# Two transformer blocks on one core: TensorE's instructions of the expert stage issued in the order of the code

## The chip, the cores and the metric

The kernel runs on one core of one Trainium2 chip. A core has five engines, each with an instruction queue that it works through in order: PE (TensorE: matrix products; its weight loads are shown as PEld), DVE (VectorE), ACT (ScalarE), POOL (GpSimd) and SP (SyncE, which here issues all loads from memory). They wait for each other through semaphores. The metric is the device time of one execution in microseconds (us), as the median of several runs.

## The reference, cut to what matters

Two blocks work on 256 tokens of 1024 features: first a block of two mixers followed by a mixture of 32 experts, then two attention layers with feed-forward parts. The change lies in the experts, where each token goes to 2 of 32:

```python
    expert = g_idx * EXPERTS_PER_GROUP + e_idx
    ...
    xb = x_pad[tok_buf].reshape(n_blocks, MOE_BLOCK, D)

    def expert_block(args):
        xbk, e = args
        return (jax.nn.silu(xbk @ w_gate[e]) * (xbk @ w_up[e])) @ w_down[e]

    yb = lax.map(expert_block, (xb, block_e)).reshape(P, D)
    y = jnp.zeros((N + 1, D), yb.dtype).at[tok_buf].add(yb * w_buf[:, None].astype(yb.dtype))
```

`w_gate` and `w_up` of one expert are 1024 x 512, `w_down` is 512 x 1024, all in 32-bit floats: 6 MiB for each expert, 192 MiB for all of them, and every expert is computed.

## The kernel before, in words

**Work of the expert stage.** Experts are taken in 16 pairs `j`; each expert has 64 token slots, so that a pair fills 128 rows. Expert `a` of a pair (0 or 1) takes columns 64a to 64a+63 of the array, and the two can run side by side. The parts are:

- `gather(quad)`, once for two pairs (four experts): picks the tokens by products with one-hot matrices `D4` (made by DVE, L1190): 32 matmuls of L1198 into eight PSUM tiles, which ACT (L1202) and DVE (L1204) scale into `xg`.
- `widen(j)`, twice for a pair (gate, then up): 16 matmuls of L1216, of which each takes 64 columns; it uses four weight tiles of 1 MiB, two for each half of the sum.
- `gated(j)`: ACT's silu of the gate product (L1222); the product with the up half is DVE's L1307.
- `turned(j)`: four transposes (L1230) of the hidden values, copied by ACT.
- `places(j)`: two transposes (L1240) and two small products (L1245) for the way back.
- `narrow(j)`: 16 matmuls of L1261 with the `down` weights (four tiles of 1 MiB), and behind them the drains: DVE scales (L1269), ACT rounds (L1270), DVE makes the rest (L1271). The results are `oh` and `ol`.
- `scatter(j)`: eight matmuls (L1280 with `oh`, L1282 with `ol`) that add a pair's result to four PSUM tiles `yp`.

Each of these 32-bit matmuls of L1216 and L1261 is two records in the trace.

**Order.** The code is a software pipeline over `j`: in the step of pair `j` it writes `gather` (for even `j`), gate half of `j`, `turned(j-1)`, `scatter(j-2)`, `places(j-1)`, up half of `j`, `narrow(j-1)`. But the code's order isn't the order on the engine: a scheduler at build time takes instructions by priority as it thinks that they come ready, and so sets the order in each queue anew. A block under `tc.manual_schedule(engines=...)` keeps the written order on the engines named.

**Groups.** Pairs 0 to 9 and 10 to 15 are two groups. Between them stands `crowded()`, a conditional block for an expert with more than 64 tokens: each engine reads a number and branches, and no instruction is moved across it. The block isn't entered with these inputs.

**Weights.** All loads are 1 MiB, issued by SP in the order of use that the code states: gate(j), up(j), down(j-1), four tiles each. 18 tiles are issued ahead of the stage; 14 of their places are then used in turn, and a further load waits for the matmuls that last read the place it is to fill, and for the load eight before it. Four of the 18 (`EARLY`) lie in buffers that the stage itself uses later; using them up starts no further load. 192 tiles are loaded in all. After them SP issues loads for the next block.

Of the kernel before, what the change touches and what calls it, by code (L numbers as in the profile page):

```python
# [16 lines left out]
OP = mybir.AluOpType  # L17
# [9 lines left out]
MORE = 2  # L27
GROUPS = (range(0, 10), range(10, 16))

EARLY = {4: "em", 3: "ay", 11: "oo", 17: "xg"}  # L30
ORDER = (0, 1, 2, 5, 6, 7, 8, 9, 10, 3, 4, 11, 12, 13, 14, 15, 16, 17)

FILL_A = (0, 0, 2, 8, 0, 2)
# [12 lines left out]
_E = mybir.EngineType  # L46
# [13 lines left out]
def block(ctx, tc, A, out, dbg=None):  # L60
    nc = tc.nc
    PE, ACT, DVE, POOL, SP = nc.tensor, nc.scalar, nc.vector, nc.gpsimd, nc.sync
# [111 lines left out]
    modc = const.tile([128, 18, 8], F32, name="modc")  # L174
# [255 lines left out]
    def bcast_cols(dst, c):  # L430

        for n in range(2):
            p = pmm()
            for a in range(4):
                PE.matmul(p[:, 128 * a:128 * a + 128], c[:, 4 * n + a:4 * n + a + 1].to_broadcast([128, 128]), ident,  # L435
                          start=a == 0, stop=a == 3, skip_group_check=True)
            ACT.activation(dst[:, 512 * n:512 * n + 512], p, AF.Copy)


    with ExitStack() as c1:  # L440
# [401 lines left out]
        op = []  # L842
# [103 lines left out]
    with ExitStack() as c2:  # L946
# [3 lines left out]
        big = lambda n: pool.tile([128, D], F32, name=n, tag="big", bufs=1)  # L950
# [144 lines left out]
        for j in ORDER:  # L1095
            rings[:] = [partial(pool.tile, tag=EARLY[j], bufs=1 + (EARLY[j] == "xg")) if j in EARLY else next(rest)]
            ahead[j] = first[j]()
# [79 lines left out]
        em = pool.tile([128, 4, 512], F32, name="em")  # L1177
        ay = pool.tile([128, 4, 512], F32, name="ay")
# [6 lines left out]
        fp = lambda t: t.rearrange("s (p f) -> s f p", f=4)  # L1185

        def gather(quad):
            D4 = pool.tile([128, 2, 4, 64], F32R, name="D4", bufs=2)
            for i in range(2):
                DVE.tensor_tensor(D4[:, i], pos[:, i, 4 * quad:4 * quad + 4, None].to_broadcast([128, 4, 64]),  # L1190
                                  slot[:, None, :].to_broadcast([128, 4, 64]), op=OP.is_equal)
            xg = pool.tile([128, KT, 256], F32, name="xg", bufs=2)
            for kt in range(KT):
                p = pmm()
                n = 0
                for i in range(2):
                    for hx in (xh, xl):
                        PE.matmul(p[:, 0:256], hx[:, i, 128 * kt:128 * kt + 128],  # L1198
                                  D4[:, i].rearrange("p e s -> p (e s)"), start=n == 0, stop=n == 3)
                        n += 1  # L1200
                if kt % 2:
                    ACT.activation(xg[:, kt, :], p[:, 0:256], AF.Identity, scale=G2r[:, kt:kt + 1], bias=S2r[:, kt:kt + 1])  # L1202
                else:
                    DVE.tensor_scalar(xg[:, kt, :], p[:, 0:256], G2r[:, kt:kt + 1], S2r[:, kt:kt + 1], op0=OP.mult, op1=OP.add)  # L1204
            S_["quad", quad] = D4, xg

        def widen(j):

            xg = S_["quad", j // 2][1]
            p = pmm()  # L1210
            for n in range(2):
                wt = [staged_moe() for a in range(2)]
                for k in range(4):
                    kt = 4 * n + k
                    for a in range(2):
                        PE.matmul(p[64 * a:64 * a + 64, :], xg[:, kt, lc(2 * j + a)], wt[a][:, k, :], start=kt == 0,  # L1216
                                  stop=kt == KT - 1, skip_group_check=True)
            return p

        def gated(j, p):  # L1220
            a4 = ac2[j % 2].rearrange("s (f p) -> s f p", f=4)
            ACT.activation(a4, fp(p), AF.Silu)  # L1222
            if j == 15:
                act_set(LNEXP)
            return a4

        def turned(j):
            p = pmm()
            for f in range(4):
                PE.transpose(p[:, 128 * f:128 * f + 128], ac2[j % 2][:, 128 * f:128 * f + 128], ident)  # L1230
            hT = hT2[j % 2].rearrange("p (f s) -> p f s", f=4)
            ACT.activation(hT, p.rearrange("p (f s) -> p f s", f=4), AF.Copy)

        def places(j):
            D4 = S_["quad", j // 2][0]
            pr_ = j % 2
            Dp = [D4[:, i, 2 * pr_:2 * pr_ + 2, :].rearrange("p e s -> p (e s)").bitcast(F32) for i in range(2)]
            p = pmm()
            for i in range(2):
                PE.transpose(p[:, 128 * i:128 * i + 128], Dp[i], ident)  # L1240
            DT = pool.tile([128, S], F32R, name="DT", bufs=2)
            ACT.activation(DT, p[:, 0:S], AF.Copy)
            p = pmm()
            for i in range(2):
                PE.matmul(p[:, 0:2], Dp[i], Wt[:, i, 2 * j:2 * j + 2], start=i == 0, stop=i == 1)  # L1245
            wsl = pool.tile([128, 1], F32, name="wsl", bufs=2)
            for a in range(2):
                DVE.tensor_copy(wsl[64 * a:64 * a + 64], p[64 * a:64 * a + 64, a:a + 1])
            S_["pair", j] = DT, wsl

        def narrow(j):
            wsl = S_["pair", j][1]
            hT = hT2[j % 2].rearrange("p (f s) -> p f s", f=4)
            pd = [pmm(), pmm()]
            for f2 in range(2):
                wt = [staged_moe() for a in range(2)]
                for b in range(2):
                    f = 2 * f2 + b
                    for n in range(2):
                        for a in range(2):  # L1260
                            PE.matmul(pd[n][64 * a:64 * a + 64, :], hT[:, f, 64 * a:64 * a + 64],  # L1261
                                      wt[a][:, b, 512 * n:512 * n + 512], start=f == 0, stop=f == 3,
                                      skip_group_check=True)
            o = pool.tile([128, 2, D], F32R, name="o", tag="oo")
            oh, ol = o[:, 0, :], o[:, 1, :]
            for n in range(2):
                ns = slice(512 * n, 512 * n + 512)
                yf = yf2[n]
                DVE.scalar_tensor_tensor(yf, pd[n], wsl, ga2[:, ns], op0=OP.mult, op1=OP.mult)  # L1269
                ACT.activation(oh[:, ns], yf, AF.Copy)  # L1270
                DVE.tensor_tensor(ol[:, ns], yf, oh[:, ns].bitcast(F32), op=OP.subtract)  # L1271
            S_["out", j] = oh, ol

        def scatter(j):
            DT = S_["pair", j][0]
            oh, ol = S_["out", j]
            for n in range(2):
                ns = slice(512 * n, 512 * n + 512)
                for i in range(2):
                    PE.matmul(yp[i][n], DT[:, 128 * i:128 * i + 128], oh[:, ns], start=j == 0, stop=False,  # L1280
                              skip_group_check=True)
                    PE.matmul(yp[i][n], DT[:, 128 * i:128 * i + 128], ol[:, ns], start=False, stop=j == 15,  # L1282
                              skip_group_check=True)
            if j == 12:

                for i in range(2):
                    for n in range(2):
                        PE.matmul(yp[i][n], ident, x_sb[:, i, 512 * n:512 * n + 512], start=False, stop=False,
                                  skip_group_check=True)
                bcast_cols(fnb, colr("fng", 8))  # L1290

        for g in GROUPS:

            before, done2 = None, None
            for j in [*g, None]:
                if j is not None:
                    if j % 2 == 0:
                        gather(j // 2)
                    a4 = gated(j, widen(j))
                if before is not None:  # L1300
                    turned(before)
                if done2 is not None:
                    scatter(done2)
                if before is not None:
                    places(before)
                if j is not None:
                    DVE.tensor_tensor(a4, a4, fp(widen(j)), op=OP.mult)  # L1307
                if j == 0:
                    ga2 = big("ga2")
                    bcast_cols(ga2, modc[:, 5, :])  # L1310
                if before is not None:
                    narrow(before)
                done2, before = before, j
            scatter(g[-1])
            if g[0] == 0:
                crowded()
        rings[:] = [slots(ring)]
# [33 lines left out]
    with ExitStack() as c3:  # L1351
# [88 lines left out]
        for ly in range(2):  # L1440
# [208 lines left out]
            for f2 in range(11):  # L1649
# [3 lines left out]
                for b in range(2):  # L1653
# [9 lines left out]
                    g, u = pgu  # L1663
# [86 lines left out]
```

## Time and profile before

| | |
|---|---|
| three runs, median | 1465.2 us (1461.68 to 1467.49) |
| the profiled execution, its own time | 1462.69 us |
| its span, first to last instruction | 1460.9 us |
| mean granted clock of TensorE | 0.981 |
| PE busy | 1376.7 us (94%) |
| DVE, ACT, POOL busy | 765.2 us, 575.1 us, 77.1 us |
| moved by the loads | 400.42 MB |
| L1216 (gate and up) | 1024 records, from 275.8 us to 725.1 us |
| L1261 (down) | 512 records, from 306.4 us to 746.0 us |

A busy PE need not be at its peak: records overlap, and a stretch counts as busy also where only one of the two column halves works. The expert stage reaches from about 270 us to about 750 us, a third of the span.

### The profile page before, as it was taken

How to read it: one execution, taken by the hardware profiler on the slowest of the kernel's cores; microseconds unless marked ns; L12 is line 12 of the kernel's file. 1: busy time of each engine (PE TensorE's matmuls, PEld its weight loads, DVE VectorE, ACT ScalarE, POOL GpSimd, SP SyncE). 2: the span in 40 equal slices, each digit the busy share in tenths (PEclk: the TensorE clock that was granted, in tenths of full speed). 3: DMA queues.
4: the chain of work that ended last, by engine and by line, in shares of the span. 5: the costliest groups of instructions: out<-in, count | busy, mean ns of one | idle time of the engine just before them, and what ended most of it. 6: DMA issues, size and time to landing. Idle time of an engine off the chain costs nothing.

```text
span 1460.9 us, 22923 instructions
## 1 busy us (share of the span) xinstructions
PE 1376.7 (94%) x9330; PEld 994.1 (68%) x9330; DVE 765.2 (52%) x1507; ACT 575.1 (39%) x1020; POOL 77.1 (5%) x79
## 2 busy tenths in 40 slices
PE   6989999799999998999979989999998999999997
PEld 5878877443443433434338867899997897799997
DVE  5648758311211111111155985888876575766665
ACT  3543014310110111101146764555556586645444
POOL 1003000100000000000010230000020001100000
PEclk9999999799999999999999999999999999999999
DMA  9926589599999999999936573878775533555540
GB/s 357 300 76 231 178 298 421 200 402 415 427 428 426 426 384 416 427 426 395 402 119 231 202 258 131 294 274 308 291 247 189 176 129 137 194 190 196 181 155 30
DMA packets 138687, 400.42 MB, mean 274 GB/s; under 512 B 6561, under 2 KB 84657, under 8 KB 114002
## 3 DMA queue, kind: packets, MB, share of 16 engines
q1 hardware_dynamic: 138578, 398.91, 71.1%
q8 instruction: 75, 1.23, 0.3%
q14 instruction: 34, 0.28, 0.1%
HBM read 397.82 MB, written 1.05 MB: 273 GB/s over the span
## 4 chain that ended last, share of the span: by engine, by line
PE 53%; DVE 3%; ACT 3%; issue 2%; POOL 0%; POOLq 0%; DVEq 0%; ACTq 0%
PE pmm L416 8%; PE pmm L417 8%; PE pmm L418 8%; PE pmm L1216 6%; PE pacc L416 5%; PE pacc L417 5%; PE pacc L418 5%; PE pmm L1261 2%; PE pmm L190 1%; PE pmm L1198 1%; PE pmm L435 1%; PE pmm L366 1%; DVE x_sb L1408 1%; PE pmm L1618 1%; PE pacc L1531 1%
## 5 line engine op out<-in xcount | busy, mean ns | idle before, releaser
L416 PE MATMUL pmm<-hh,whi 128*128 128x256 f32 (+1 forms) x1040 | 295.4, 284 | 2.0 <-ACT whi L167 2.0
L418 PE MATMUL pmm<-hh,wlo 128*128 128x256 f32 (+1 forms) x1040 | 296.2, 285 | 0.2 <-DVE wlo L168 0.2
L417 PE MATMUL pmm<-hl,whi 128*128 128x256 f32 (+1 forms) x1040 | 294.6, 283 | 0.0
L1216 PE MATMUL pmm<-wruns,xg 128*64 128x512 f32 x1024 | 237.1, 595 | 0.0
L168 DVE TENSOR_TENSOR wlo<-wcols,whi 128x1024 fp32r<-128x1024 f32 (+1 forms) x130 | 168.3, 1299 | 97.5 <-ACT whi L167 97.1
L416 PEld LDWEIGHTS pmm<-hh,whi 128*128 128x128 f32 (+1 forms) x1040 | 196.9, 189 | 8.5 <-issue 3.6
L417 PEld LDWEIGHTS pmm<-hl,whi 128*128 128x128 f32 (+1 forms) x1040 | 196.1, 189 | 1.4
L418 PEld LDWEIGHTS pmm<-hh,wlo 128*128 128x128 f32 (+1 forms) x1040 | 196.4, 189 | 0.6 <-DVE wlo L168 0.4
L167 ACT ACTIVATE whi<-wcols 128x1024 fp32r<-128x1024 f32 (+1 forms) x130 | 136.0, 1052 | 116.3 <-PE pmm L417 89.1
L1216 PEld LDWEIGHTS pmm<-wruns,xg 128*64 128x64 f32 x1024 | 73.9, 137 | 141.3 <-issue 139.2
L1261 PE MATMUL pmm<-wruns,em 128*64 128x512 f32 x512 | 138.4, 596 | 0.0
L168 DVE TENSOR_TENSOR wlo<-wrows,whi 128x1024 fp32r<-128x1024 f32 x87 | 108.1, 1249 | 56.6 <-ACT whi L167 56.2
L167 ACT ACTIVATE whi<-wrows 128x1024 fp32r<-128x1024 f32 x87 | 91.6, 1061 | 92.3 <-PE pmm L417 46.7
L1307 DVE TENSOR_TENSOR ay<-ay,pmm 128x512 f32<-128x512 f32 x16 | 11.0, 688 | 184.6 <-PE pmm L1216 184.6
L1261 PEld LDWEIGHTS pmm<-wruns,em 128*64 128x64 f32 x512 | 44.0, 137 | 73.5 <-issue 71.0
L1270 ACT ACTIVATE o<-ay 128x512 fp32r<-128x512 f32 x32 | 20.1, 629 | 160.1 <-DVE ay L1269 160.1
L417 PE MATMUL pacc<-wlo,ah 128*128 128x512 f32 x176 | 69.2, 393 | 0.0
L416 PE MATMUL pacc<-whi,ah 128*128 128x512 f32 x176 | 68.9, 391 | 0.0
L418 PE MATMUL pacc<-whi,al 128*128 128x512 f32 x176 | 68.6, 393 | 0.0
L1269 DVE SCALAR_TENSOR_TENSOR ay<-pmm,wsl,ga 128x512 f32<-128x512 f32 x32 | 24.0, 751 | 82.9 <-PE pmm L1261 81.2
L1202 ACT ACTIVATE xg<-pmm,GS 128x256 f32<-128x256 f32 x32 | 18.0, 562 | 88.0 <-PE pmm L1198 78.2
L1222 ACT ACTIVATE ay<-pmm 128x512 f32<-128x512 f32 x16 | 9.6, 598 | 108.9 <-PE pmm L1216 108.9
(533 smaller groups left out, 2198.8 us busy)
## 6 DMA issues: line engine op xcount, KB each, us to landing
wruns<-in_moe_w_gate_dram SPq DMA_DIRECT2D x64, 1024.0 KB, 11.7
wruns<-in_moe_w_up_dram SPq DMA_DIRECT2D x64, 1024.0 KB, 13.5
wruns<-in_moe_w_down_dram SPq DMA_DIRECT2D x64, 1024.0 KB, 13.6
wrows<-in_w_mod_dram SPq DMA_DIRECT2D x48, 1024.0 KB, 7.2
wcols<-in_w_ffn_gate_dram SPq DMA_DIRECT2D x22, 1024.0 KB, 5.1
wcols<-in_w_ffn_up_dram SPq DMA_DIRECT2D x22, 1024.0 KB, 7.4
wrows<-in_w_ffn_down_dram SPq DMA_DIRECT2D x22, 1024.0 KB, 5.2
wrows<-in_ada_w_dram SPq DMA_DIRECT2D x16, 1024.0 KB, 7.4
```

Of the source, the lines that this page charges most:

```text
L167: ACT.activation(hi, src, AF.Copy)
L168: (POOL if ahead else DVE).tensor_tensor(lo, src, hi.bitcast(F32), op=OP.subtract)
L190: PE.matmul(p[32 * g:32 * g + 32, 0:n].rearrange("p (a j) -> p a j", j=32), lhsT, groups(rhs)[:, g], start=first, stop=last, skip_group_ch ...
L366: PE.matmul(p, src[:, i, 128 * kt:128 * kt + 128], dg[i], start=True, stop=True)
L416: PE.matmul(p, a[0], b[0], start=first, stop=False, skip_group_check=True)
L417: PE.matmul(p, a[0], b[1], start=False, stop=False, skip_group_check=True)
L418: PE.matmul(p, a[1], b[0], start=False, stop=last, skip_group_check=True)
L1202: ACT.activation(xg[:, kt, :], p[:, 0:256], AF.Identity, scale=G2r[:, kt:kt + 1], bias=S2r[:, kt:kt + 1])
L1216: PE.matmul(p[64 * a:64 * a + 64, :], xg[:, kt, lc(2 * j + a)], wt[a][:, k, :], start=kt == 0, stop=kt == KT - 1, skip_group_check=True)
L1261: PE.matmul(pd[n][64 * a:64 * a + 64, :], hT[:, f, 64 * a:64 * a + 64], wt[a][:, b, 512 * n:512 * n + 512], start=f == 0, stop=f == 3, ski ...
L1269: DVE.scalar_tensor_tensor(yf, pd[n], wsl, ga2[:, ns], op0=OP.mult, op1=OP.mult)
L1270: ACT.activation(oh[:, ns], yf, AF.Copy)
```

## The change

All of TensorE's instructions of the two group loops stand under `manual_schedule`, so they are issued as written. The code is written in another order, too: the `gather` of the next two pairs stands between the up half of an odd pair and the `narrow` ahead of it (before, ahead of the gate half of an even pair); in a group's last step `turned` comes behind `scatter` and `places`. Of the loads issued ahead, tile 12 instead of tile 17 lies in the second `xg` buffer, since that buffer is now filled before tile 17 is used.

```diff
-EARLY = {4: "em", 3: "ay", 11: "oo", 17: "xg"}
+EARLY = {4: "em", 3: "ay", 11: "oo", 12: "xg"}
...
         for g in GROUPS:
 
-            before, done2 = None, None
-            for j in [*g, None]:
-                if j is not None:
-                    if j % 2 == 0:
-                        gather(j // 2)
-                    a4 = gated(j, widen(j))
-                if before is not None:
-                    turned(before)
-                if done2 is not None:
-                    scatter(done2)
-                if before is not None:
-                    places(before)
-                if j is not None:
-                    DVE.tensor_tensor(a4, a4, fp(widen(j)), op=OP.mult)
-                if j == 0:
-                    ga2 = big("ga2")
-                    bcast_cols(ga2, modc[:, 5, :])
-                if before is not None:
-                    narrow(before)
-                done2, before = before, j
-            scatter(g[-1])
+            with tc.manual_schedule(engines={_E.PE}):
+                before, done2 = None, None
+                gather(g[0] // 2)
+                for j in [*g, None]:
+                    if j is not None:
+                        a4 = gated(j, widen(j))
+                        if before is not None:
+                            turned(before)
+                    if done2 is not None:
+                        scatter(done2)
+                    if before is not None:
+                        places(before)
+                    if j is not None:
+                        DVE.tensor_tensor(a4, a4, fp(widen(j)), op=OP.mult)
+                    else:
+                        turned(before)
+                    if j == 0:
+                        ga2 = big("ga2")
+                        bcast_cols(ga2, modc[:, 5, :])
+                    if before is not None:
+                        if j is not None and j % 2 and j + 1 in g:
+                            gather((j + 1) // 2)
+                        narrow(before)
+                    done2, before = before, j
+                scatter(g[-1])
             if g[0] == 0:
                 crowded()
```

What stands in PE's queue in the middle of the first group, before the change, where the next quad is gathered (`D` is the one-hot matrix, `em` the transposed hidden values, `ay` the hidden values; each "..." is 8 to 10 more rows of L1198 of the same kind):

```order
L1216 MATMUL pmm<-wruns,xg 64x512 x31
L1261 MATMUL pmm<-wruns,em 64x512 x2
L1198 MATMUL pmm<-D_3885,xh 128x256
...
L1261 MATMUL pmm<-wruns,em 64x512 x6
...
L1261 MATMUL pmm<-wruns,em 64x512 x2
...
L1261 MATMUL pmm<-wruns,em 64x512 x6
...
L1280 MATMUL pacc<-o,DT 128x512 x2
L1216 MATMUL pmm<-wruns,xg 64x512
L1230 MATMUL pmm<-ident,ay 128x128 x4
L1282 MATMUL pacc<-o,DT 128x512 x2
```

The gate half of the next pair stands with the up half of this one (31 of 32 together, one behind the drains), and `narrow` is cut into four pieces with `gather` between them. The same engine at the same place in the program, with the change ("..." is the rest of the 32 rows of L1198):

```order
L1216 MATMUL pmm<-wruns,xg 64x512 x16
L1198 MATMUL pmm<-D_3854,xh 128x256
...
L1261 MATMUL pmm<-wruns,em 64x512 x16
L1216 MATMUL pmm<-wruns,xg 64x512 x16
L1230 MATMUL pmm<-ident,ay 128x128 x4
L1280 MATMUL pacc<-o,DT 128x512
L1282 MATMUL pacc<-o,DT 128x512
```

Up half, gather, `narrow` and the next gate half now stand each in one piece, and in the order in which their weights are loaded. Within each piece the two column halves alternate from matmul to matmul, as the code writes them; before, the scheduler had put two matmuls of the same half one behind the other in most of `narrow`.

The second place is ACT's queue at the end of the stage, where the last pair's results are rounded (L1270) and the first weights of the next block are split (L167). Before:

```order
L1242 ACTIVATE DT<-pmm 128x256
L1270 ACTIVATE o<-ay 128x512 x4
L167 ACTIVATE hilo<-wrows 128x1024 x2
L294 ACTIVATE sqj,ssx_5374<-pacc 128x512
L294 ACTIVATE sqj,sst_5376<-tf 128x512
```

And with the change:

```order
L1232 ACTIVATE em<-pmm 128x512
L1270 ACTIVATE o<-ay 128x512
L167 ACTIVATE hilo<-wrows 128x1024
L1270 ACTIVATE o<-ay 128x512
L167 ACTIVATE hilo<-wrows 128x1024
L294 ACTIVATE sqj,ssx_5380<-pacc 128x512
```

One split of the next block's weights now stands between the two last roundings.

## Rows read from the trace of the kernel before

**Rows 1.** The page, 40 equal slices of the span: GB/s moved by the loads.

```profile
GB/s 357 300 76 231 178 298 421 200 402 415 427 428 426 426 384 416 427 426 395 402 119 231 202 258 131 294 274 308 291 247 189 176 129 137 194 190 196 181 155 30
```

**Rows 2.** Stretches: length, busy PE, PEld, DVE, ACT, POOL (instructions); clock, DMA share, GB/s.

```profile
280.00:300.00 20.00, 20.00 (x106) 8.36 (x104) 0.72 (x2) 2.93 (x6) 0.00 (x0) 1.00 0.93 347
300.00:320.00 20.00, 20.00 (x107) 9.24 (x107) 5.57 (x11) 3.69 (x8) 0.00 (x0) 1.00 1.01 420
320.00:340.00 20.00, 20.00 (x99) 8.05 (x97) 1.76 (x5) 1.53 (x3) 0.00 (x0) 1.00 0.99 397
433.73:493.63 59.90, 58.39 (x261) 23.81 (x260) 10.52 (x20) 7.72 (x15) 0.00 (x0) 1.00 1.01 426
540.00:560.00 20.00, 15.90 (x60) 5.96 (x56) 6.35 (x10) 2.52 (x4) 0.00 (x0) 1.00 0.82 334
...
680.00:700.00 20.00, 20.00 (x90) 7.93 (x87) 0.31 (x2) 2.07 (x4) 0.00 (x0) 1.00 0.85 327
716.00:736.00 20.00, 19.47 (x88) 7.06 (x84) 1.75 (x4) 2.75 (x4) 0.00 (x0) 1.00 0.87 363
```

**Rows 3.** Timeline of PE, start and duration, first pairs, whose pieces stand whole.

```profile
275.83 13.95 PE L1216 MATMUL pmm<-wruns,xg 128*64 128x512 f32 x64
...
341.55 7.04 PE L1216 MATMUL pmm<-wruns,xg 128*64 128x512 f32 x32
...
358.45 7.09 PE L1261 MATMUL pmm<-wruns,em 128*64 128x512 f32 x32
365.47 0.39 PE L1198 MATMUL pmm<-D,xh 128*128 128x256 f32 x1
...
369.72 3.65 PE L1216 MATMUL pmm<-wruns,xg 128*64 128x512 f32 x16
```

**Rows 4.** Timeline of PE in the middle of the first group (brackets: idle before, releaser).

```profile
433.73 13.52 PE L1216 MATMUL pmm<-wruns,xg 128*64 128x512 f32 x61
...
455.25 0.73 PE L1280 MATMUL pacc<-o,DT 128*128 128x512 f32 x2 [0.71 <-ACT o L1270]
...
476.12 3.65 PE L1261 MATMUL pmm<-wruns,em 128*64 128x512 f32 x12
...
493.63 13.52 PE L1216 MATMUL pmm<-wruns,xg 128*64 128x512 f32 x61
```

**Rows 5.** Timeline of PE's weight loads in the same quad.

```profile
462.08 0.14 PEld L1216 LDWEIGHTS pmm<-wruns,xg 128*64 128x64 f32 x2 [0.29 <-issue]
...
478.31 0.14 PEld L1261 LDWEIGHTS pmm<-wruns,em 128*64 128x64 f32 x1 [0.29 <-issue]
...
483.24 0.19 PEld L1198 LDWEIGHTS pmm<-D,xh 128*128 128x128 f32 x1 [0.81 <-issue]
```

**Rows 6.** Timeline of SP, the issue of loads at the end of the stage.

```profile
718.47 0.39 SPq L143 DMA_DIRECT2D wrows<-in_w_qkv_dram  x1
719.31 3.80 SPq L143 DMA_DIRECT2D wrows<-in_w_mod_dram  x3
```

**Rows 7.** Timeline of PE and ACT between the groups and at the end.

```profile
556.68 0.63 PE L1282 MATMUL pacc<-o,DT 128*128 128x512 f32 x2
...
563.38 0.55 PE L1198 MATMUL pmm<-D,xh 128*128 128x256 f32 x1 [6.06 <-PEq L1120]
...
569.27 14.81 PE L1216 MATMUL pmm<-wruns,xg 128*64 128x512 f32 x66
...
739.98 7.09 PE L1261 MATMUL pmm<-wruns,em 128*64 128x512 f32 x30
...
748.43 1.99 ACT L167 ACTIVATE hilo<-wrows 128x1024 fp32r<-128x1024 f32 x2
```

**Rows 8.** A stretch between the groups (columns as in rows 2).

```profile
562.00:564.00 2.00, 0.62 (x3) 0.65 (x4) 0.76 (x2) 0.00 (x0) 0.00 (x0) 0.50 1.00 422
```

**Rows 9.** Single instruction lines: the identity products of the second group, L1288 and L435.

```profile
L1288 PE MATMUL pacc<-x_sb,ident x8: 592/592/697, 678.7 to 686.6; 128*128 128x512 f32 x8
L435 PE MATMUL pmm<-ident,par x16: 275/275/376, 690.7 to 692.5; 128*128 128x128 f32 x16
```

## The prediction

> **What bounds the kernel now.** First the slices of the page [rows 1]: in the expert stage (from the ninth slice to the twentieth) the loads run at 384 to 428 GB/s, nowhere else for so long; the dips among these are what to look at. The stretches [rows 2] then show both sides at once: in one quad (two pairs) from 433.73 to 493.63 us PE is busy for 58.39 of 59.90 us, while the loads move 426 GB/s at a share of 1.01. So neither waits visibly for the other, and the question is which of them is only filled up.
>
> The timeline of PE answers it. Early in the stage, where each part stands whole, a pair takes 23.92 us (341.55 to 365.47), and a gather up to 4.25 us (365.47 to 369.72, with one scatter product in it) [rows 3]. Two pairs and a gather would be 52.1 us. In the middle of the group the same work takes 59.90 us [rows 4]: 7.8 us more. The loads of 24 tiles (24 x 1.0486 MB = 25.17 MB) at 426 GB/s take 59.1 us. PE is thus 0.8 us slower than the loads in a quad, with 7.8 us that aren't work. Where they go is read from the weight loads [rows 5]: in L1216 two go in each 0.43 us, one for each column half; in the cut `narrow` of L1261 most come singly at the same step, so one half of the array stands idle, and at each change between 64 and 128 columns 0.81 us pass. That is why twelve shown records of L1261 take 3.65 us [rows 4], where 32 take 7.09 [rows 3]. In each pair PE also waits 0.71 us for ACT's L1270, the first drain of `narrow`, since scatter comes right behind it [rows 4].
>
> At the end the slower one shows: from 716 to 736 us the loads move 363 x 20 = 7.26 MB [rows 2], 6.9 tiles, of which the last four are the next block's [rows 6]. So 2.9 tiles of the experts are left at 716, and the last lands at about 716 + 2.9 x 2.46 = 723 us. PE ends its last `narrow` at 739.98 + 7.09 = 747.07 us [rows 7], 24 us later. Loads also fell short twice because the places weren't freed: 334 GB/s in 540 to 560 and 327 in 680 to 700, which is 4.3 and 4.7 us of loads at 426 [rows 2].
>
> **The change, part by part.**
>
> *PE's work.* Nothing is added or removed: the same matmuls in another order. The clean pair of [rows 3] is the new order, piece by piece, with no wait in it, so I take 23.92 us for a pair; in the new place the gather's results have the whole `narrow` (7.0 us) to reach `xg`, and ACT and DVE are mostly idle there (10.52 and 7.72 us busy of 59.90 [rows 2]). A gather of 4.2 us is the upper value, 3.9 without the scatter product. Waits that the trace doesn't show in this order: at least 0 (the clean pair), at most the 0.71 us of [rows 4] in each pair, 11 us in all. I take 0, since scatter now stands a whole gate half (7.0 us) behind the drain that it waited for.
>
> PE alone would then run: from 275.83 us [rows 3], ten pairs 239.2, four gathers 16.8, the broadcast beside pair 0 about 2 and the last drain 3: group one ends at 537. Group two is six pairs (143.5), two gathers (8.4) and the identity products, eight records at 0.43 us and sixteen in 1.8 (together 5.6) [rows 9]: 157.5 us.
>
> *The loads.* All 192 tiles must still come, and they can't come faster than at about 426 GB/s: 2.46 us each. By 340 us the loads have moved (347 + 420 + 397) x 20 = 23.28 MB, 22.2 tiles [rows 2], which with the 18 issued ahead leaves 151.8. At 2.46 us they take 373.6 us: 713.6 us, if they never stop. One new stop I count: the first gather of the loop (4.2 us) now stands ahead of the first `narrow`, so the places of tiles 16 and 17 come free 4.2 us later. It costs 0 if enough loads are queued to cover it, and 4.2 if none are; no row shows the queue there, so I take the middle, 2.1. That gives 715.7.
>
> Is PE ahead of this? Tile 119, the last of group one, is the 79.8th of these and lands at 340 + 2.1 + 79.8 x 2.46 = 538.4 us; PE alone would be done by then. From there: a landing delay of 1 us (I bound it by 0 and 2), half a `narrow` (3.5), the drains (about 3), then 11.96 us from the last scatter through the branch to the first L1216 (557.31 to 569.27 [rows 7]): 557.9. With 157.5 us of work PE would end at 715.4, while the loads need half a `narrow` behind the last tile: 715.7 + 1 + 3.5 = 720.2 us. The loads decide, by some 5 us, and PE's waits below 0.8 us a pair in group two cost nothing. The pause at the branch is covered: 14 places are 34 us of loads.
>
> *The end.* ACT's L167 now stands between the last two L1270: 1.0 us [rows 7], of which nothing hides most, because the last scatter waits for the second. I take 1.0 (bounds 0 and 1.0; if its load is late, 2.5 more). What follows, the next block, starts when `narrow` and its drains are done, and moves as a whole.
>
> *Two edits at nothing.* `turned` behind `scatter` in a group's last step: the same five short matmul groups, covered by the wait for tiles there. The buffer of tile 12 instead of 17: one place fewer, none more.
>
> **Sum.** 747.07 - 720.2 - 1.0 = 25.9 us. The profiled execution's own 1462.69 us becomes 1436.8; it lies 2.5 us under the median of the runs, so for the median 1439.3, say **1439 us**. The stop (0 to 4.2), the landing (0 to 2), the last L167 (0 to 3.5) and a GB/s or two move this by 4 us down and 6 up: 1435 to 1445.
>
> The Trainium skill, in DMA: Bandwidth & Descriptors (Where 436 GB/s comes from), puts the ceiling of the loads at 435 GB/s, and says that for loads from memory about 358 bind. By 435 the 151.8 tiles would take an estimated 366 us and the end would come 7.7 us earlier; by 358 they would take 445 us. The trace disagrees with 358 (426 over a whole quad) and reaches 428 in a slice at most [rows 1].
>
> **The rivals.**
>
> *PE still waits in its new order.* The scheduler had moved the gate half ahead for a reason, perhaps for drains. If each pair has 1.5 us of waits (twice the 0.71 of [rows 4]), group one ends at 537 + 15 = 552, 6 us after what the loads allow (538.4 + 7.5), and group two is 9 us longer: 715.4 + 15 = 730.4 instead of 720.2: 1449 us. Against it: the clean pair shows none. Chance 0.15.
>
> *The loads were the limit all along.* For it: 426 GB/s for whole quads. Then only the two dips go, 9.0 us: 1456 us. Against it: PE ends 24 us behind the last tile. Chance 0.08.
>
> *The wait for tiles slows PE's clock (slower than before).* PE will now wait for tiles, by (59.1 - 52.1) / 12 = 0.6 us for each half of a part. After 6.06 us without work [rows 7] the granted clock stood at 0.50, 1.2 GHz instead of 2.4 [rows 8]. If that came with the short waits, the three 7 us parts of a pair would take 14 each: 21 us more for each pair so slowed. Two such pairs cost 42 us, and the result is 1439 + 42 = 1481 us; from (25.9 + 7.3) / 21 = 1.6 pairs on it is more than 0.5% slower. Against it: with waits of 0.71 us in each pair the clock stayed at 1.00 [rows 2]. Chance 0.03. The Trainium skill, in TensorE: Matmul & The Clock Gate (HAM oscillation — how this bites in real kernels), tells of a kernel whose waits for each weight slice brought the slow clock back every time; here the waits are shorter than any that the trace shows at 0.50.
>
> *The loads run faster than 426 once PE never holds them.* With 434 GB/s 151.8 tiles take 366.8 us, 6.8 less: 1432 us, with PE 2 us behind them. Chance 0.06.
>
> **How the numbers follow.** My forecast has 0.68. Range: 1431 takes in the faster loads and the lower bounds, 1453 the new waits; left out are the dips alone (0.08), the slow clock (0.03) and some tails: about 0.17. The likeliest case's own range is the 1435 to 1445 above. About 0.5%, 7.3 us, is what a measurement of this kernel tells from no change: under 1457.9 lie the forecast, the waits, the faster loads and most of the 0.08: 0.94 faster, 0.03 the same, 0.03 slower.
>
> **What would show it.** In the changed kernel's trace: weight loads of L1261 in twos at 0.43 us; pairs of about 24 us up to roughly 460 us and then quads at 59 us, PE waiting on loads of `wruns` rather than on L1270; no dip in the loads from 345 us to the end of the stage; PE's last `narrow` ending 3 to 5 us behind the last tile, near 720 us. Wrong would be: a quad above 60 us, loads below 420 GB/s in the middle, waits of PE on ACT or DVE of more than 0.8 us a pair, or a clock below 1.00 inside a group.

## The result

1442.44 us, median of four runs (1441.75 to 1445.49), against 1465.4 us before (1461.68 to 1467.49, four runs): a ratio of 0.985, with a 95% interval of 0.9826 to 0.9875, some 23 us gained. The prediction of 1439 us, with its range of 1431 to 1453, was right. The traced execution is the slowest of the four (1445.49 us, its span 1443.7), and reaches the experts 3 us later than that of before: the first L1216 starts at 278.81 us, not 275.83. So positions are compared from the first L1216 on, and I call "the stage" the time from there to the first L366 of the next block: 481.9 us before (757.71 - 275.83), 462.1 after (740.91 - 278.81), a gain of 19.8 us. The rest of the two spans differs by 2.6 us the other way, in work that the change doesn't touch.

### The profile page after: what moved, and what is told of

It reads as the page before. It is cut to its first block, busy times and chain, and to the rows that moved or that the text cites. A ratio compares the mean times of both kernels' runs of the same rounds, so it can differ in the third digit from the quotient of the medians.

```text
span 1443.7 us, 22926 instructions
## 1 busy us (share of the span) xinstructions
PE 1356.1 (94%) x9330; PEld 1002.3 (69%) x9330; DVE 763.9 (53%) x1507; ACT 576.5 (40%) x1020; POOL 77.9 (5%) x79
## 4 chain that ended last, share of the span: by engine, by line
PE 44%; DMA 9%; DVE 3%; ACT 3%; issue 1%; POOL 0%; POOLq 0%; DVEq 0%; SPq 0%; ACTq 0%
PE pmm L416 8%; PE pmm L417 8%; PE pmm L418 8%; PE pacc L416 5%; PE pacc L417 5%; PE pacc L418 5%; DMA wruns<-in_moe_w_gate_dram 4%; DMA wruns<-in_moe_w_down_dram 3%; DMA wruns<-in_moe_w_up_dram 2%; PE pmm L190 1%; PE pmm L1261 1%; ACT sqj L294 1%; PE pmm L366 1%; PE pmm L1622 1%; PE pmm L435 1%
## 5 line engine op out<-in xcount | busy, mean ns | idle before, releaser
L1216 PE MATMUL pmm<-wruns,xg 128*64 128x512 f32 x1024 | 233.1, 595 | 7.1 <-DMA wruns<-in_moe_w_gate_dram 7.1
L168 DVE TENSOR_TENSOR wlo<-wcols,whi 128x1024 fp32r<-128x1024 f32 (+1 forms) x130 | 168.4, 1300 | 99.3 <-ACT whi L167 98.8
L167 ACT ACTIVATE whi<-wcols 128x1024 fp32r<-128x1024 f32 (+1 forms) x130 | 136.1, 1053 | 119.0 <-PE pmm L417 91.7
L1216 PEld LDWEIGHTS pmm<-wruns,xg 128*64 128x64 f32 x1024 | 81.8, 137 | 141.1 <-issue 115.8
L168 DVE TENSOR_TENSOR wlo<-wrows,whi 128x1024 fp32r<-128x1024 f32 x87 | 108.1, 1248 | 56.3 <-ACT whi L167 55.9
L167 ACT ACTIVATE whi<-wrows 128x1024 fp32r<-128x1024 f32 x87 | 91.7, 1061 | 90.5 <-PE pmm L417 45.5
L1261 PE MATMUL pmm<-wruns,em 128*64 128x512 f32 x512 | 118.4, 595 | 7.2 <-DMA wruns<-in_moe_w_down_dram 5.7
L1261 PEld LDWEIGHTS pmm<-wruns,em 128*64 128x64 f32 x512 | 38.5, 137 | 79.3 <-issue 62.4
L1270 ACT ACTIVATE o<-ay 128x512 fp32r<-128x512 f32 x32 | 20.2, 631 | 177.5 <-DVE ay L1269 177.5
L1248 DVE COPY wsl<-pmm 64x1 f32<-64x1 f32 x32 | 5.0, 156 | 130.7 <-PE pmm L1245 130.4
```

The lines of the kernel that those rows point to most:

```text
L167: ACT.activation(hi, src, AF.Copy)
L168: (POOL if ahead else DVE).tensor_tensor(lo, src, hi.bitcast(F32), op=OP.subtract)
```

## The profile after

The slices of the page, GB/s moved by the loads, to be held against [rows 1]:

```profile
GB/s 361 295 69 251 164 274 380 226 365 426 426 427 426 427 427 402 391 426 427 427 246 252 196 228 146 336 276 311 286 248 181 172 117 149 184 196 196 178 150 30
```

From the tenth slice to the twentieth one dip is left, 402 and 391. Before there were two, 384 and 395.

PE's timeline early in the stage (start, duration), which answers to [rows 3]:

```profile
320.79 7.04 PE L1216 MATMUL pmm<-wruns,xg 128*64 128x512 f32 x32
327.76 0.66 PE L1230 MATMUL pmm<-ident,ay 128*128 128x128 f32 x4
...
330.76 7.09 PE L1216 MATMUL pmm<-wruns,xg 128*64 128x512 f32 x32
337.68 7.04 PE L1261 MATMUL pmm<-wruns,em 128*64 128x512 f32 x32
344.54 7.04 PE L1216 MATMUL pmm<-wruns,xg 128*64 128x512 f32 x32
...
365.55 7.09 PE L1261 MATMUL pmm<-wruns,em 128*64 128x512 f32 x32
372.47 4.03 PE L1216 MATMUL pmm<-wruns,xg 128*64 128x512 f32 x18
```

All pieces stand whole (the x18 of the last row is only where this view ends). A pair takes 23.75 us (320.79 to 344.54), one with a gather 27.93, a quad 51.68. Further on PE waits for loads, first at 453 us:

```profile
447.90 4.62 PE L1216 MATMUL pmm<-wruns,xg 128*64 128x512 f32 x18
453.74 3.65 PE L1216 MATMUL pmm<-wruns,xg 128*64 128x512 f32 x14 [1.21 <-DMA wruns<-in_moe_w_gate_dram]
```

The stretches of the core (columns as in [rows 2]): two with waits for loads, the stop between the groups, and the end.

```profile
500.00:520.00 20.00, 16.41 (x77) 6.82 (x74) 3.10 (x6) 2.83 (x5) 0.00 (x0) 1.00 1.01 426
...
560.00:580.00 20.00, 20.00 (x103) 13.71 (x103) 2.32 (x4) 2.60 (x5) 0.00 (x0) 0.99 0.82 335
680.00:700.00 20.00, 20.00 (x93) 7.59 (x89) 3.48 (x5) 2.10 (x4) 0.00 (x0) 1.00 1.01 427
```

In 500 to 520 PE is busy for 16.41 us only, at clock 1.00. The dip at 680 to 700 (327 before) is gone; the one between the groups, 334 before, is still there with 335. Its cause is in SP's queue. These are the instructions of the branch line L1120 (count, duration in ns, first and last start), before:

```profile
L1120 SPq EVENT_SEMAPHORE  x8: 17/17/17, 531.7 to 546.5; - x8
L1120 SPq COMPARE_BRANCH  x1: 50/50/50, 529.4 to 529.4; - x1
```

and after:

```profile
L1120 SPq EVENT_SEMAPHORE  x8: 17/17/17, 575.5 to 578.3; - x8
...
L1120 PEldq COMPARE_BRANCH  x1: 6126/6126/6126, 551.2 to 551.2; - x1
L1120 PEldq EVENT_SEMAPHORE  x1: 51/51/51, 557.3 to 557.3; - x1
L1120 SPq COMPARE_BRANCH  x1: 50/50/50, 559.3 to 559.3; - x1
```

SP compares at 559.3 and gets past the eight semaphores at 578.3. They are those of its eight outstanding loads: as the program is written, SP leaves the conditional block only when every load that it has issued has landed. The landing times in the trace agree: before, the loads issued from 523.03 to 529.06 us land at 539.18, 541.61, 544.03 and 546.45, and a wait of SP ends within 0.02 us of each. The queue of loads runs dry and starts anew. Before, this lasted from 529.4 to 546.5. The prediction had taken that dip for places that weren't free. (PE passes a branch of its own here, which takes 6.1 us, and 6.0 before.)

The end of the stage on PE (answers to [rows 7]):

```profile
715.16 3.65 PE L1261 MATMUL pmm<-wruns,em 128*64 128x512 f32 x14 [1.14 <-DMA wruns<-in_moe_w_down_dram]
719.51 0.49 PE L1280 MATMUL pacc<-o,DT 128*128 128x512 f32 x1 [0.71 <-ACT o L1270]
720.25 0.50 PE L1282 MATMUL pacc<-o,DT 128*128 128x512 f32 x1 [0.24 <-DVE o L1271]
...
722.57 0.64 PE L1230 MATMUL pmm<-ident,ay 128*128 128x128 f32 x4
723.89 7.09 PE L1261 MATMUL pmm<-wruns,em 128*64 128x512 f32 x32 [0.69 <-ACT em L1232]
731.70 0.51 PE L1280 MATMUL pacc<-o,DT 128*128 128x512 f32 x1 [0.72 <-ACT o L1270]
...
735.65 0.80 PE L1282 MATMUL pacc<-o,DT 128*128 128x512 f32 x1 [1.98 <-DVE o L1271]
```

The last wait for a load ends at 715.16. Behind it come half a `narrow`, `scatter`, `places`, `turned` and a whole `narrow`, with three waits for drains (0.71, 0.24, 0.69). The last `narrow` ends at 730.98. DVE's last L1271 comes late:

```profile
731.73 0.68 DVE L1271 TENSOR_TENSOR o<-ay,o 128x512 fp32r<-128x512 f32 x1
732.99 0.69 DVE L1333 TENSOR_TENSOR tf<-pacc,em 128x512 f32<-128x512 f32 x1 [0.59 <-PE pacc L1282]
733.60 1.99 DVE L1271 TENSOR_TENSOR o<-ay,o 128x512 fp32r<-128x512 f32 x1
```

It takes 1.99 us in place of 0.68, beside POOL's split of the next block's weights (L168, 732.67 to 737.82).

## The experiments

**How they are read.** The theory: PE's new order frees it, and from then on the loads bound the stage; what is left to gain are stops of the loads and the chain at the end. Repeated runs of one kernel lie up to 6.5 us apart (the kernel before: 1459.53 to 1466.03), and chips differ a little, so that medians tell some 3 us from nothing; smaller steps are read from the stage of the traced execution, one for each kernel.

| kernel | median, us | ratio to before, 95% | stage, us |
|---|---|---|---|
| before | 1465.4 | | 481.9 |
| after | 1442.4 | 0.9826 to 0.9875 | 462.1 |
| e1_fixed_old | 1439.6 | 0.9817 to 0.9870 | 459.1 |
| e2_order_only | 1453.0 | 0.9902 to 0.9955 | 471.1 |
| e3_fewer_loads | 1418.3 | 0.9671 to 0.9723 | 436.5 |
| e4_halves_apart | 1449.1 | 0.9876 to 0.9929 | 469.0 |
| e5_no_branch | 1440.8 | 0.9822 to 0.9848 | 457.4 |
| e6_pool_loads | 1440.1 | 0.9816 to 0.9843 | 457.9 |
| e7_tail | 1445.9 | 0.9860 to 0.9890 | 462.1 |
| e8_gather1 | 1441.6 | 0.9826 to 0.9854 | 461.4 |
| e9_old_pool | 1440.3 | 0.9817 to 0.9843 | 458.9 |
| e10_old_pool_split | 1442.4 | 0.9830 to 0.9862 | 459.7 |
| e11_turned_first | 1444.6 | 0.9849 to 0.9881 | 461.8 |
| e12_old_pool_at | 1438.3 | 0.9815 to 0.9844 | 458.7 |

**One part alone: the fixed order (e1_fixed_old).** The loop of before, put under `manual_schedule`:

```diff
+            with tc.manual_schedule(engines={_E.PE}):
                 before, done2 = None, None
                 for j in [*g, None]:
```

> TensorE's instructions of the expert stage in the order written, but the code in its old order: each gather ahead of the gate half of an even pair, `turned` ahead of `scatter` in a group's last step, tile 17 in the early buffer. Theory (the gain is the whole pieces of `narrow` and the alternating column halves, and from the middle on the loads bound the stage, so that where the gather stands is covered): 1442 us, 1440 to 1446. Rival (the gather between the pair's two halves is what gains): 1450 to 1465.

1439.6 us. The fixed order alone gives the whole gain. The other edits gain nothing on top of it: the stage is even 3.0 us shorter than after's. Part of that is early: over the first 60 us of the stage the loads average 359 GB/s, 349 in after (from 20 to 40 us 408 for 358), which is 1.4 us of loads. Where the rest comes from stays open.

**The other part alone (e2_order_only).** The code of after without the `with`.

> The code in its new order, but the scheduler still free to set TensorE's queue. It cuts `narrow` again: 48 places where two matmuls of the same column half follow each other (52 in the kernel before, none after). Theory: 1455 to 1466, most of the gain gone. Rival (the new place of the gather gains): 1440 to 1450.

1453.0 us, better than expected: half the gain. The scheduler still cuts pieces and hoists part of the gate half, but now the gather cuts `widen` into three pieces and leaves `narrow` whole: a pair with its gather takes 31.42 us (462.79 to 494.21) against 34.18 before (459.45 to 493.63) and 27.93 after; one without takes the same 25.7 us as before. PE never waits for loads here. So PE bounds this kernel, and the new code order is worth about 12 us while the scheduler is free, and nothing once the order is fixed.

**Is it the loads? (e3_fewer_loads).** The second half of `narrow` uses the tiles of the first:

```diff
-        dn_runs = lambda j: [... for f2 in range(2) for a in range(2)]
+        dn_runs = lambda j: [... for f2 in range(1) for a in range(2)]
...
-                wt = [staged_moe() for a in range(2)]
+                wt = wt if f2 else [staged_moe() for a in range(2)]
```

> The kernel after, with a sixth of the experts' loads left out: the second half of each `narrow` computes with the tiles of its first half again, so the result is another one. TensorE's instructions are the same. Theory (the loads at 426 GB/s bound the second half of the stage, TensorE alone would be some 13 us faster: 7.1 us of waits for loads at L1216 and 5.7 at L1261 in the profile after): 1429 us, 1425 to 1433. Rival (TensorE waits for something that goes with the places or the branch, not with the bytes): 1438 to 1444.

1418.3 us: 24 us less with the same instructions on PE, so the loads do bound the kernel after, and by twice what was expected. The groups of lines show why, after first, then this kernel (busy us, mean ns of one | idle before):

```profile
L1216 PE MATMUL pmm<-wruns,xg 128*64 128x512 f32 x1024 | 233.1, 595 | 7.1 <-DMA wruns<-in_moe_w_gate_dram 7.1
L1261 PE MATMUL pmm<-wruns,em 128*64 128x512 f32 x512 | 118.4, 595 | 7.2 <-DMA wruns<-in_moe_w_down_dram 5.7 <-ACT em L1232 1.4
```

```profile
L1216 PE MATMUL pmm<-wruns,xg 128*64 128x512 f32 x1024 | 225.5, 594 | 0.0
L1261 PE MATMUL pmm<-wruns,em 128*64 128x512 f32 x512 | 113.0, 594 | 1.4 <-ACT em L1232 1.4
```

Beside the 12.8 us of idle time before records, 13.0 us of "busy" are gone (233.1 + 118.4 - 225.5 - 113.0). A wait for a tile within a piece is partly shown as busy PE: at 453.74 us PE shows 1.21 us of idle time, its weight load 2.09. In the stage of after the weight loads show 28.2 us of idle time ended by loads, in 19 gaps that otherwise take 0.29 us each. The two parts on PE are 25.8 us together; the stage got 25.6 shorter.

**The column halves (e4_halves_apart).**

```diff
-                for b in range(2):
-                    f = 2 * f2 + b
-                    for n in range(2):
-                        for a in range(2):
+                for a in range(2):
+                    for b in range(2):
+                        f = 2 * f2 + b
+                        for n in range(2):
```

> The kernel after, with only the loops within `narrow` exchanged: four matmuls of one column half, then four of the other, instead of alternating. Same matmuls, whole pieces, no cut. Theory (two neighbours on different halves run side by side, two on the same half do not): 13 steps of 0.87 us in place of 8, so a `narrow` takes 11.3 us in place of 7.1; 16 x 4.3 = 69 us more, less the 13 us that TensorE now waits for loads: 1498 us, 1480 to 1510. Rival (the cutting and the changes between 64 and 128 columns cost the time, not the halves): 1441 to 1446.

1449.1 us, 7 more and not 56: the theory of this experiment fell, and so did its rival. PE's timeline where `narrow` meets the next gate half:

```profile
338.34 7.63 PE L1261 MATMUL pmm<-wruns,em 128*64 128x512 f32 x29
345.39 0.64 PE L1216 MATMUL pmm<-wruns,xg 128*64 128x512 f32 x1
345.81 0.59 PE L1261 MATMUL pmm<-wruns,em 128*64 128x512 f32 x1
...
346.73 7.40 PE L1216 MATMUL pmm<-wruns,xg 128*64 128x512 f32 x29
354.06 0.66 PE L1230 MATMUL pmm<-ident,ay 128*128 128x128 f32 x4
```

One half is ahead by a few records and goes on into the gate half, while the other finishes `narrow`. The two run side by side all the same. The lag is paid once, where work of 128 columns follows, as the weight loads show:

```profile
463.13 0.14 PEld L1216 LDWEIGHTS pmm<-wruns,xg 128*64 128x64 f32 x1 [0.29 <-issue]
463.56 0.14 PEld L1216 LDWEIGHTS pmm<-wruns,xg 128*64 128x64 f32 x1 [0.29 <-issue]
463.99 0.14 PEld L1216 LDWEIGHTS pmm<-wruns,xg 128*64 128x64 f32 x1 [0.29 <-issue]
464.94 0.14 PEld L1230 LDWEIGHTS pmm<-ident,ay 128*128 128x128 f32 x1 [0.81 <-issue]
```

A pair (from L1230 to L1230) takes 25.63 us (328.43 to 354.06) for 23.75 in after (327.76 to 351.51): 1.9 us, not 4.3. Sixteen times 1.88 us on the stage of e3_fewer_loads, where PE doesn't wait for loads, is 436.5 + 30.1 = 466.6 us; measured 469.0. So same-half neighbours need not cost anything by themselves: they leave one half behind, and PE pays for that where the piece ends. That each cut in the kernel before is paid in this way is concluded, not measured: no run cuts the pieces and keeps the halves alternating.

**The branch (e5_no_branch, e6_pool_loads).** In the first the call of `crowded()` is left out; in the second

```diff
-                ahead.append(t())
+                ahead.append(t(q=POOL) if 120 <= k < 132 else t())
```

> The kernel after without the conditional block `crowded()` between the groups (it isn't entered with these inputs). Theory (SP's branch waits for the landing of all its outstanding loads, so the queue of loads runs empty and starts anew, some 4.5 us of loads, and the stage is bound by loads): 4.5 us less than the kernel after, 3 to 7, no dip in the loads near 580 us. Rival (the dip comes from places that are not free; the branch itself is covered): 0 to 1 us less, the dip stays.

> The kernel after, with the twelve loads that follow SP's branch issued by POOL, which has passed its own branch before the stage begins. Theory (loads can go on while SP waits at the branch for its own to land): the dip near 580 us goes, 3 to 5 us less than the kernel after. Rival (the queue empties all the same since both queues share the engines and end together, or POOL's issue is slower): 0, or up to 5 us more.

The stage is 4.7 and 4.2 us shorter than after's, as expected for the stop. The medians are only 1.6 and 2.4 less, short of the expected 3 to 7 and 3 to 5; they point the same way, but can't tell it from nothing. From 280 to 300 us into the stage the loads of after move 356 GB/s; here are the same 20 us without the branch, then with POOL's loads:

```profile
558.35:578.35 20.00, 20.00 (x98) 8.00 (x96) 1.00 (x3) 2.06 (x4) 0.00 (x0) 1.00 1.01 428
```

```profile
554.99:574.99 20.00, 20.00 (x104) 9.59 (x105) 2.87 (x5) 2.86 (x5) 4.43 (x8) 0.95 1.01 424
```

SP still sat at its branch in the second (555.6 to 581.5), and the loads didn't stop. So the stop is SP's branch, which waits for the landing of its own loads. e5_no_branch also takes away PE's own 6.1 us at the branch; e6_pool_loads keeps them (5.9 us) and gains nearly as much, so it isn't they that count.

**The tail (e7_tail, e11_turned_first).** In e7 the last step of a group is `turned`, `places`, `narrow` and then both scatters; in e11 only `turned` moves back ahead of `scatter` and `places`.

> The kernel after, with the last step of each group written as `turned`, `places`, `narrow`, then the scatter of the pair before and the last scatter. Theory (behind the last wait for loads TensorE does scatter, places, turned and a whole `narrow` with 1.6 us of waits for drains, while the last tile lands near 725 us and needs only half a `narrow` behind it): the last `narrow` ends 2.4 us earlier, and the scatter of the pair before covers the wait for the last drains: 2 to 4 us less than the kernel after. Rival (the end is set by ACT, DVE and POOL, which round and split there): 0 to 1 us less.

> The kernel after with one part undone: in a group's last step `turned` stands ahead of `scatter` and `places` again. Theory (`turned` covers the drains that scatter waits for, 0.71 and 0.24 us, and scatter covers ACT's copy of the transposed values, 0.69 us, at a place where TensorE is the bound): the stage is 1.4 us shorter than after's, the branch not on the path; 1 to 2 us less. Rival (`turned` is late itself, since DVE's product of the two halves comes late): 0.

In e7 the last `narrow` ends 2.1 us earlier, as expected (450.07 us from the first L1216, 452.18 in after), but the next block then takes 12.0 us to begin, not 9.9, and nothing is won. ACT's timeline:

```profile
726.90 2.01 ACT L167 ACTIVATE hilo<-wrows 128x1024 fp32r<-128x1024 f32 x2 [6.65 <-DMA wrows<-in_w_qkv_dram]
730.11 1.15 ACT L1270 ACTIVATE o<-ay 128x512 fp32r<-128x512 f32 x2 [1.20 <-PE pacc L1282]
```

The rounding waits for PE's L1282 of the pair before: there is one buffer `o`, and `scatter` has to have read it. Ahead of the last `narrow`, `scatter` frees that buffer in time. In e11 the way from the last wait for loads to the last `narrow` is 7.62 us (715.49 to 723.11), 8.73 in after (715.16 to 723.89): 1.1 us, the expected 1.4 nearly. The stage gains 0.3 of it in its one trace; the median, 2.2 us more, doesn't resolve it.

**The first gather (e8_gather1).** For `j == 1`, `gather(1)` behind `narrow(0)`.

> The kernel after, with the first gather of the loop behind the first `narrow` instead of ahead of it, so that the places of tiles 16 and 17 come free 4 us earlier. Theory (the early dip of the loads at 316 to 320 us is this wait, and what the loads lose early they never get back): 2 us less than the kernel after, 1 to 4, no dip there. Rival (the loads catch up, or the gather's results then hold up the gate half): within 1 us of the kernel after.

The stage is 0.7 us shorter. From 40 to 60 us the loads move 426 GB/s for 412; over the first 60 us it is 0.6 MB more, 1.4 us of loads, part of which is lost again at the branch. The place of the gather costs about a microsecond.

**Both together (e9_old_pool, e12_old_pool_at).** e1_fixed_old with POOL's loads; the second differs in one line:

```diff
-                ahead.append(t(q=POOL) if 120 <= k < 132 else t())
+                ahead.append(t(q=POOL) if 109 <= k < 121 else t())
```

> TensorE's fixed order with the code in its old order (as in e1_fixed_old), and the twelve loads behind SP's branch issued by POOL (as in e6_pool_loads). Theory (both remove stops of the loads, which bound the stage, so they add: 3.0 and 4.2 us of the stage): 7 us less than the kernel after, 1435 us, 1433 to 1438, ratio to the kernel before 0.980. Rival (one slack covers both, or TensorE becomes the bound): no better than the better of the two, 1439 to 1440.

> As e9_old_pool, but with the twelve loads by POOL at the right place: in the code's old order SP branches behind load 123, not 134, so the twelve start there (in e9_old_pool they came behind the stop, which stayed: 327 GB/s in its 20 us). Five of them stand ahead of POOL's own branch. Theory (the stop goes, as in e6_pool_loads, and adds to what the old order gains early): 4 us less than e1_fixed_old, 1435.5 us, 1433 to 1438, no stretch below 415 GB/s between 540 and 560 us. Rival (POOL now waits at its own branch for its five loads, and the stop is only moved): 1439 to 1441, a dip of like size a few us later.

Neither adds up. In e9 the twelve loads were at the wrong place: with the old order SP branches behind load 123. In e12 SP waited from 524.1 to 554.4, POOL's loads kept 424 GB/s until 553 us, and then the loads fell to 385 and 394 in the two stretches of 20 us behind: its rival, the stop only moved. The last loads of POOL wait for places:

```profile
549.31 0.53 POOL L149 DMA_DIRECT2D wruns<-in_moe_w_up_dram  x1 [4.37 <-issue]
563.25 0.53 POOL L149 DMA_DIRECT2D wruns<-in_moe_w_up_dram  x1 [13.41 <-PE pmm L1216]
```

1438.3 us is the lowest median, but its interval overlaps after's. No version is shown to beat the kernel after; e1, e5, e6, e9 and e12 lie 2 to 4 us under it, which these runs can't tell from it.

**The last drains (e10_old_pool_split).**

```diff
+        gate[:] = [S_["last"].ins]
         rows = rows_ahead(A["w_qkv_2"][0][:, 2048:3072], PREL)
+        gate[:] = []
```

> As e9_old_pool, and the next block's first two weight splits (ACT's L167, then POOL's L168) queued behind ACT's last rounding of the last pair. Theory (the split between the two last L1270 delays the second by 0.9 us, and POOL's L168 beside it makes DVE's last L1271 take 1.99 us for 0.69): the way from the last `narrow` to the next block falls from 9.7 to 7.3 us, so 2 to 2.5 us less than e9_old_pool. Rival (the splits are needed just as soon, so the next block waits for them): within 0.5 us of e9_old_pool.

This was missed: the way to the next block got longer, 10.7 us for 10.0. The drains went as expected: two L1271 in 1.47 us, and the last scatter ended 3.4 us behind `narrow`, 6.3 in e9. But POOL's split now ran beside what DVE does next:

```profile
728.76 2.70 DVE L1332 TENSOR_TENSOR tf<-pacc,em 128x512 f32<-128x512 f32 x4
731.55 3.27 DVE L1358 TENSOR_SCALAR lt<-jp 128x128 fp32r<-128x128 f32 x1
733.82 1.07 DVE L1360 CAST one<-ones 128x128 fp32r<-128x128 f32 x1
```

L1358 took 3.27 us (the same instruction 0.62 in after), and the chain of small DVE instructions that L366 waits for stood behind it. That is the order of the kernel before [rows 7], and nearly its 10.6 us; there, too, this instruction ran beside POOL's split (749.55 to 754.22):

```profile
751.95 3.27 DVE L1355 TENSOR_SCALAR lt<-jp 128x128 fp32r<-128x128 f32 x1
```

In both places that were tried POOL's split costs DVE something, and beside L1271 it costs less.

## Why the prediction was right, and where it was off

- **PE's work, 23.92 us a pair and no waits: right.** 23.75 measured. PE waits for a drain only in each group's last step. Its reason stands in part: it put the loss down to matmuls that "come singly" and to the switches. e4_halves_apart shows that the order of halves is paid where a piece ends, so the cuts make it cost; how much of the loss is single matmuls and how much switches, no run separates.
- **PE alone ahead of the loads: right in kind, mis-sized.** The prediction's own terms put PE alone at 537 + 12 + 157.5 = 706.5 us; e3_fewer_loads, shifted to the same first L1216, ends its last `narrow` at 705.0. But "by some 5 us" compared group two alone, from a start that the loads had set. The loads cost the kernel after 24 us. The landing delay of 1 us in that sum stands in no row: at the last wait the load's landing is recorded at 715.11 us, and PE goes on at 715.16.
- **The loads.** In the first 60 us of the stage they moved 21.0 MB, before 21.6: 1.5 us for the early stop (2.1 taken, bounds 0 to 4.2). The rate is 427. **The step that failed is the pause at the branch, "covered":** the places were free, but SP didn't issue. (427 - 356 + 427 - 390) x 20 us is 2.2 MB, 5.0 us, in the two stretches of after from 558.81 us, where SP compares and waits; in e5_no_branch the same stretches have 428 and 426. Only the dip at 680 to 700 went. In 440 us from the first L1216 the loads of after move 181.0 MB, those of before 179.6: they are 3 us ahead, not the forecast's 7 (723 to 715.7).
- **Half a `narrow` behind the last tile: too short.** PE was behind already: scatter, places, `turned` and a whole `narrow` with 1.6 us of waits. e7_tail gets 2.1 us of that.
- **L167, 1.0 us more: it became 0.7 less.** From the last `narrow` to L366 it is 9.9 us, 10.6 before. The second L1270 did start late, at 732.50, and L1271 was slowed, but POOL's split came earlier and spared the DVE instruction that it had slowed before; e10_old_pool_split puts it back, and gets 10.7.
- **The sum.** The last `narrow` was to end 26.9 us earlier, and ended 19.1 us earlier (from the first L1216: 452.18 for 471.24). Of the missing 7.8, some 4 to 5 are the branch and 2.1 the tail; about 1 stays open. The larger part of the gain isn't faster loading at all. By the landing times in the traces the last tile came at 725.4 us before, not at the forecast's 723, and PE ended its last `narrow` 21.7 us behind it, not 24. After, it came at 724.9, and PE ended 6.1 us behind it (e7_tail still waits for this tile 446.4 us into the stage, for the 452.2 at which `narrow` ends). So 15.6 of the 19.1 us are PE's lag, and 3.5 the loads.
- **Luck.** In the traces the stage gained 19.8 us for a forecast of 25.9. The medians differ by 23, nearer to the forecast, since the trace of before is 2.7 us below its median and that of after 3.0 above; which part of this belongs to the stage, no run tells. A sign of being wrong also came true: loads below 420 GB/s in the middle (356 and 390 at the branch).
- **The rivals.** New waits of PE in each pair: none. Loads the limit all along (1456): the result lies 14 us under it, and e2_order_only, with the same loads, takes 1453 us without a wait of PE for them. The slow clock: 1.00 in 500 to 520, with waits of up to 1.3 us each. The Trainium skill, in TensorE: Matmul & The Clock Gate (HAM oscillation — how this bites in real kernels), tells of waits for the next slice of the operand that streams through (here the weights) that bring the slow clock back; here, with these waits, the rows show none. Loads at 434, a rate that no run shows: they stayed at 427.

## What to carry to other kernels

Where PE and the loads seem equally busy over a stretch, look at how far PE ends behind the last load: that lag, not the rate in the middle, was what a better order could win here. A branch on the engine that issues loads was paid in loads, since the queue ran dry however many buffers were free; loads issued by an engine that is past its branch went on (e6_pool_loads), as long as their places were free (e12_old_pool_at). And before a drain, a scatter or a split is moved, look for the single buffer and for the neighbour engine that it will run beside.

## What was not expected of the hardware

- Two column halves run on at a distance: with four matmuls of one half and then four of the other a pair costs 1.9 us more, not 4.3.
- A stage in which PE shows 12.8 us of waits for loads lost 24 to 26 to them (e3_fewer_loads).
- SP, with eight loads of 1 MiB outstanding, sat at a branch for 19.0 us (after) until they had landed, and the loads fell from 427 to 356 GB/s in those 20 us.
- DVE beside POOL's split: L1271 took 1.99 us for 0.68 alone; L1358 took 3.27, for 0.62 in after and 0.23 in e7_tail, where that split was over. The Trainium skill, in GPSIMD Engine Reference (1. Specifications), says that the two share their memory interfaces, and that DVE instructions with two inputs there, or in a two-port mode, contend. L1271, with two inputs, agrees; L1358 has one, and no run here shows its mode.
